# A list schedule for every engine, in place of program order, in a two-layer hybrid block

## The chip, the core and the metric

The kernel runs on one core of one Trainium2 chip. The metric is the device time of one execution in microseconds (us); the figure to go by is the median of a few runs. The core has a tensor engine (PE), a vector engine (DVE), a scalar engine (ACT), GpSimd (POOL), a sync engine (SP) that here issues nearly all loads, and 16 DMA engines. Each engine takes its instructions from a queue of its own, in order; semaphores make an instruction wait for work of another engine. A matrix product takes its operands from SBUF and accumulates in PSUM, of which the kernel keeps six tiles for its products: `mm_66` to `mm_69`, and the two larger ones `ax_70` and `ax_71`.

## The reference

Two layers work on 256 context tokens and 512 latent tokens, 1024 channels wide, all in float32. One input projection feeds three groups of heads side by side; their outputs are joined and projected; then comes an MLP. Each half ends in a gated residual and a LayerNorm. The second layer keeps only the latent tokens.

```python
def layer(x, c, ...):
    p = modulate(x, shift, scale) @ w_in             # one projection, split in three
    a = chunk_token_mlp(p_a)                         # gated token mixing in chunks of 128
    b = gqa(p_b)                                     # softmax attention, 6 query heads, rotary
    d = gated_delta_rule(conv(q), conv(k), conv(v))  # chunks of 64, a state passed on, two directions
    x = layer_norm(alpha * x + gate * (concat(a, b, d * gate_z) @ w_out))
    h = square(relu(modulate(x, ...) @ w_up))        # 1024 -> 4096
    return layer_norm(alpha * x + gate2 * (h @ w_down))
```

## The kernel before

**Tiles and stages.** Tokens go in groups of 128, channels in groups of 128. A float32 operand of a large product is split into a rounded half and a rest (`whi`, `wlo` for a weight; `xh`, `xl`, `x2xh`, `x2xl`, `hh`, `hl` for activations), and `mm3` (line 385) forms each product as three: high with high, high with low, low with high. ACT makes the rounded half and DVE the rest (`split`, line 381). So every weight goes from DRAM into `wraw`, then over ACT (`whi`) and DVE (`wlo`) to PE. Per layer the stages are: modulation and projection; convolutions and gates of the delta rule; three rounds `p` of `dn_prep` (a triangular inverse built by 31 dependent DVE steps), `makes` and `scans` of 64x64 products in the four quarters of the array (`kv,TT`, `S,rP`, `rwu,A`, `id,qd`, `kd,rwu`); attention beside them (scores `akh,qs` and `akl,qs` in an `ax` tile, transposes of `ape`, then `apT,ava`, the product of weights and values, on half of the array); the output projection; and the MLP, whose first product goes through the `mm` tiles and whose second collects in `ax_70` and `ax_71` and is added to `acc` by DVE.

**What sets the order.** Every engine call goes through `_Engine.call` (line 213), so all instructions carry L213 and are told apart by tile names. The stages are Python generators, and class `Flow` (line 30) runs them side by side: it keeps an estimated clock for each engine from hand-written costs, resumes the generator whose time is earliest (less `BIAS` for the delta-rule chains), and lends out PSUM tiles. So a generator writes its instructions in small bunches. What comes out is one program order, which the tile framework's own priorities turn into the engines' queues. PSUM tiles and buffers are assigned there, while the program is written.

```python
            for s in self.live:
                t = self.when(s)
                if t is not None and (best is None or (t - s[5], s[1]) < best[:2]):
                    best = (t - s[5], s[1], t, s)
```

Of the kernel before, what the change touches and what calls it, by code (L numbers as in the profile page):

```python
# [9 lines left out]
F32R = mybir.dt.float32r  # L10
# [3 lines left out]
PSUM = bass.MemoryType.PSUM  # L14
DRAM = bass.MemoryType.DRAM

P = 128
# [22 lines left out]
class Flow:  # L40
# [8 lines left out]
    def __init__(self, tc):  # L49
        self.tc = tc  # L50
        self.free = {}
        self.ready = {}
        self.done = {}
        self.live = []
        self.count = 0
        self.last = 0.0
        self.slots = {}
        self.spare = {}
        self.lent = {}
# [7 lines left out]
    @staticmethod  # L67
    def width(a):
        n = 1
        for s in a.shape[1:]:  # L70
            n *= s
        return n
# [150 lines left out]
            setattr(self, k, _Engine(flow, k, getattr(nc, k)))  # L223


def _tb(v):

    return 1 - v if v < 2 else 7 - v
# [62 lines left out]
class K:  # L291
    def __init__(self, ctx, tc, d, dump=None):
        self.tc = tc
        self.flow = Flow(tc)
        self.nc = _Core(tc.nc, self.flow)
        self.d = d
        self.dump = dump
        self.ctx = ctx
        self.open_ = []


    def open(self, name, side="left", space=None):
        kw = {} if space is None else {"space": space}
        cm = self.tc.tile_pool(name=name, bufs=1, side=side, reuse_waits="tile", **kw)
        p = cm.__enter__()
        self.open_.append((p, cm))
        return p

    def close(self, *pools):
        for p in pools:  # L310
            i = next(i for i, (q, _) in enumerate(self.open_) if q is p)
            self.open_.pop(i)[1].__exit__(None, None, None)

    def setup(self):
        nc, tc, ctx, d = self.nc, self.tc, self.ctx, self.d
# [348 lines left out]
def _body(ctx, tc, d, out, dump=None, stop=None):  # L664
    K_ = Kernel(ctx, tc, d, dump)
    K_.run(out, stop)
    for p, cm in reversed(K_.open_):
        cm.__exit__(None, None, None)

# [17 lines left out]
class Kernel(K):  # L687
# [784 lines left out]
    def dn_make(self, l, p, v, qkv, G, A, TT, r):  # L1472
# [5 lines left out]
        kds, ks, egc, be, E = G["kds"], G["ks"], G["egc"], G["be"], G["E"]  # L1478
        hs = slice(2 * p, 2 * p + 2)
        td = (v, _tb(v))  # L1480
        a0 = 0 if l == 0 else 2
        he = lambda a: a.rearrange("p t (h e) -> p t h e", e=HD)
# [59 lines left out]
    def dn_scan(self, l, p, v, A, r, S, o):  # L1542

        nc, sc = self.nc, self.dn
        need = l == 0 or v > 1
        a0 = 0 if l == 0 else 2
        td = (v, _tb(v))
        mm = nc.tensor.matmul
        halves = [_half(f) for f in range(2)]
# [405 lines left out]
```

## Time and profile before

| | before |
|---|---|
| median of 3 runs | 2041.31 us (2038.36 to 2041.98) |
| profiled execution | 2039.17 us, span 2037.4 us |
| granted TensorE clock, mean | 0.950 |
| PE busy | 1859.2 us, 91% |
| DVE busy | 1284.2 us, 63% |
| ACT busy | 854.5 us, 42% |
| POOL busy | 279.2 us, 14% |
| DMA | 204.44 MB, mean 100 GB/s |
| chain that ended last | PE 61%, DVE 18%, issue 7%, ACT 5%, POOL 4%, DMA 3% |

Busy times are sums over instructions, with overlaps counted once; the profiled execution's own time is its span and about 2 us around it. By stages, in us from the span's start: modulation and projection of layer 0 to 104, convolutions and first delta-rule work to 309, mixers to 538, output projection to 616, MLP to 1179 (PE without a pause), layer 1's mixers to 1609, its output projection to 1663, its MLP to 2027, and a last LayerNorm to 2037.4. The granted clock is the share of full speed that TensorE was given: 1.00 is 2.4 GHz, and a stretch at 1.2 GHz counts as 0.5.

### The profile page before, as it was taken

Reading aid. Unit: us, or ns where it says so; the run is one execution under the profiler, and the core shown is the slowest. Engines: PE = TensorE matmul, PEld = TensorE weight load, DVE = VectorE, ACT = ScalarE, POOL = GpSimd, SP = SyncE. Lnnn points to the kernel's source line nnn. Section 1 sums busy time; section 2 is a strip of 40 time slices with the busy share of each in tenths; the row PEclk is TensorE's granted clock in tenths of the full one; section 3 lists DMA queues with packets and bytes.
Section 4 is the critical chain, followed back from the end, with each engine's and each line's share of the span. In section 5 each row is a group of like instructions: output and inputs, shape, how many; then the busy total and the mean of one; then the engine's idle time right before and its main releaser. Section 6 shows DMA issues by size and latency. Waiting matters only on the chain.

```text
span 2037.4 us, 35195 instructions
## 1 busy us (share of the span) xinstructions
PE 1859.2 (91%) x14496; PEld 1519.5 (75%) x14496; DVE 1284.2 (63%) x2165; ACT 854.5 (42%) x1607; POOL 279.2 (14%) x479
## 2 busy tenths in 40 slices
PE   6999887898898999999999989988778879999997
PEld 2778675566678878888888777877666668888886
DVE  4668786765587245464457776888785575544555
ACT  3434435456546322322232274443655545323331
POOL 1111215431021000000000111111522020000001
PEclk8989889989999999999999979987997989999999
DMA  8211015313326323242355242100000544322331
GB/s 284 93 58 50 27 37 175 120 31 118 107 96 226 99 83 115 83 155 74 113 165 185 84 147 89 62 29 21 27 27 6 189 164 136 103 83 83 114 104 52
DMA packets 74060, 204.44 MB, mean 100 GB/s; under 512 B 9730, under 2 KB 23938, under 8 KB 73900
## 3 DMA queue, kind: packets, MB, share of 16 engines
q1 hardware_dynamic: 62764, 184.51, 27.9%
q10 hardware_dynamic: 11136, 17.70, 2.3%
q8 instruction: 113, 1.85, 0.4%
q14 instruction: 47, 0.39, 0.1%
HBM read 184.38 MB, written 17.79 MB: 99 GB/s over the span
## 4 chain that ended last, share of the span: by engine, by line
PE 61%; DVE 18%; issue 7%; ACT 5%; POOL 4%; DMA 3%; SPq 0%; ACTq 0%; POOLq 0%; DVEq 0%
PE mm L213 37%; PE ax L213 25%; DVE cacc L213 2%; DVE Xx L213 2%; DVE tm L213 2%; DVE wlo L213 2%; POOL crn L213 2%; DVE M L213 1%; DMA wraw<-in_w_up 1%; POOL rs L213 1%; DVE anm L213 1%; ACT ape L213 1%; DVE st L213 1%; POOL arn L213 1%; ACT osq L213 1%
## 5 line engine op out<-in xcount | busy, mean ns | idle before, releaser
L213 ACT ACTIVATE whi<-wraw 128x1024 fp32r<-128x1024 f32 (+2 forms) x188 | 194.6, 1050 | 443.1 <-PE ax L213 287.7
L213 DVE TENSOR_TENSOR wlo<-wraw,whi 128x1024 fp32r<-128x1024 f32 (+2 forms) x188 | 226.6, 1212 | 236.5 <-ACT whi L213 235.7
L213 PE MATMUL mm<-x2xh,whi 128*128 128x256 f32 (+1 forms) x832 | 287.7, 346 | 12.3 <-ACT whi L213 11.2
L213 PE MATMUL mm<-x2xl,whi 128*128 128x256 f32 (+1 forms) x832 | 287.0, 345 | 0.0
L213 PE MATMUL mm<-x2xh,wlo 128*128 128x256 f32 (+1 forms) x832 | 285.4, 343 | 0.7 <-DVE wlo L213 0.7
L213 PE MATMUL ax<-whi,hh 128*128 128x512 f32 x640 | 251.4, 393 | 0.1
L213 PE MATMUL ax<-wlo,hh 128*128 128x512 f32 x640 | 250.2, 391 | 0.0
L213 PE MATMUL ax<-whi,hl 128*128 128x512 f32 x640 | 250.1, 391 | 0.0
L213 PEld LDWEIGHTS mm<-x2xh,whi 128*128 128x128 f32 x832 | 159.7, 192 | 34.6 <-ACT whi L213 12.0
L213 DVE TENSOR_TENSOR acc<-acc,ax 128x1024 f32<-128x1024 f32 x68 | 83.0, 1220 | 148.3 <-PE ax L213 148.2
L213 PEld LDWEIGHTS mm<-x2xh,wlo 128*128 128x128 f32 x832 | 159.0, 191 | 20.0 <-DVE wlo L213 1.1
L213 PEld LDWEIGHTS mm<-x2xl,whi 128*128 128x128 f32 x832 | 159.7, 192 | 17.5
L213 PEld LDWEIGHTS ax<-whi,hh 128*128 128x128 f32 x640 | 120.2, 188 | 29.6 <-ACT hh L213 5.6
L213 PEld LDWEIGHTS ax<-whi,hl 128*128 128x128 f32 x640 | 120.2, 188 | 27.3 <-DVE hl L213 2.9
L213 PEld LDWEIGHTS ax<-wlo,hh 128*128 128x128 f32 x640 | 120.3, 188 | 26.9 <-issue 2.6
L213 POOL TENSOR_SCALAR rs<-mv 128x1 f32<-128x1 f32 x52 | 33.1, 638 | 702.6 <-DVE mv L213 701.4
L213 DVE SCALAR_TENSOR_TENSOR acc<-modw,cz,acc 128x1024 f32<-128x1024 f32 x80 | 101.2, 1282 | 7.6 <-DMA acc<-in_mod_b 4.6
L213 ACT ACTIVATE rl<-mm 128x256 f32<-128x256 f32 (+1 forms) x104 | 50.7, 490 | 131.4 <-PE mm L213 131.4
L213 POOL MEMSET acc<- 128x1024 f32 x10 | 9.5, 955 | 468.9 <-PE mm L213 468.9
L213 DVE TENSOR_TENSOR hl<-rl,hh 128x768 fp32r<-128x768 f32 (+2 forms) x76 | 54.5, 717 | 29.7 <-ACT hh L213 29.7
L213 DVE TENSOR_REDUCE anm<-ax 128x1 f32<-128x768 f32 (+1 forms) x60 | 50.6, 848 | 33.3 <-PE ax L213 33.2
L213 DVE SCALAR_TENSOR_TENSOR cacc<-cb,cw,cacc 128x772 f32<-128x772 f32 (+1 forms) x72 | 70.0, 975 | 0.7 <-ACT cacc L213 0.2
(255 smaller groups left out, 4127.1 us busy)
## 6 DMA issues: line engine op xcount, KB each, us to landing
modw<-in_mod_w SPq DMA_DIRECT2D x80, 512.0 KB
wraw<-in_w_up SPq DMA_DIRECT2D x64, 512.0 KB
wraw<-in_w_down SPq DMA_DIRECT2D x64, 512.0 KB
wraw<-in_w_ch SPq DMA_DIRECT2D x22, 512.0 KB
modw<-in_mod_w SPq DMA_DIRECT2D x32, 256.0 KB
wraw<-in_w_out SPq DMA_DIRECT2D x16, 512.0 KB
x_d<-xt ACTq DMA_DIRECT2D x16, 512.0 KB
xt<-x_d SPq DMA_DIRECT2D x14, 512.0 KB
```

Source lines behind the costliest of these rows:

```text
L213: return f(*args, **kw)
```

## The change

When the whole program is written, a new class `Order` goes over it once more. It takes all instructions, builds the graph of what must precede what (`graph`, from the memory that each reads and writes, from PSUM tiles and from the buffers of pools, whose openings and closings new wrappers record), gives each a cost (`costs`), and works out the longest path from each to the end (`tail`). `schedule` then simulates the engines and fills each one's queue: of the instructions that are ready, the one with the longest path to the end goes first. On PE two rules are added. Products on disjoint parts of the array that have the same operand names (one kind) form a unit and are issued one behind the other (`units`). And among the first `LOOK` (16) candidates, one of the same kind as the last product gets a bonus of `STICK` (5000 ns of path). No instruction, tile, shape or buffer is added, removed or altered; the order on each engine's queue is fixed by dependencies without semaphores.

```diff
+    SAME, OTHER = 110.0, 220.0
+    LOOK, STICK, LATE, SWITCH = 16, 5000.0, 20.0, 250.0
...
+        for i in pe:
+            x = self.ins[i]
+            self.kind[i] = tuple(a.bass_ap.tensor.name.split("_")[0].rstrip("0123456789") for a in (*x.ins, *x.outs) if hasattr(a, "bass_ap"))
+            part = len(self.cells[i]) < 16
+            if unit and (not part or used & set(self.cells[i]) or any(newest(j) > unit[0] and j not in unit for j in self.pred[i]) or self.kind[i] != self.kind[unit[0]]):
+                close()
+                unit, used = [], set()
...
+    def schedule(self, key):
...
+            elif e == E.PE:
+                some = [heapq.heappop(avail[e]) for _ in range(min(len(avail[e]), self.LOOK))]
+                worth = lambda c: (c[0] - self.STICK * (self.kind[c[1]] == last) + self.LATE * max(0.0, max(cell[q] for q in self.cells[c[1]]) - t), c[1])
+                pick = min(some, key=worth)
...
+            else:
+                k, i = heapq.heappop(avail[e])
...
+    def apply(self):
+        far = self.tail()
+        out = self.schedule([-f for f in far])
+        dep = mybir.DependencyInfo(mybir.DependencyClass.NoSync, mybir.DependencyReason.DATA)
+        for e, seq in out.items():
+            for a, b in zip(seq, seq[1:]):
+                self.tc.add_manual_dep(self.ins[b], self.ins[a].name, dep)
...
 def _body(ctx, tc, d, out, dump=None, stop=None):
     K_ = Kernel(ctx, tc, d, dump)
     K_.run(out, stop)
+    Order(tc, K_.pools).apply()
```

**First place.** PE in the projection of layer 0, around the product of the delta rule's gates `g` with the triangle `tri`. A row is a position in the queue, the tile written, its operands, the tile's shape and how many in a row. Before:

```order
226 L213 MATMUL mm_66<-xh,wlo 128x256
227 L213 MATMUL mm_68<-xh,whi 128x512
228 L213 MATMUL mm_68<-xl,whi 128x512
229 L213 MATMUL mm_68<-xh,wlo 128x512
230 L213 MATMUL mm_69<-g,tri 128x36 x4
231 L213 MATMUL ax_70<-tri,g 6x128 x6
232 L213 MATMUL mm_66<-xh,whi 128x256
```

And after the change:

```order
253 L213 MATMUL mm_67<-xh,wlo 128x512
254 L213 MATMUL mm_66<-xh,wlo 128x256
255 L213 MATMUL mm_68<-xh,wlo 128x512
256 L213 MATMUL mm_66<-xh,whi 128x256
257 L213 MATMUL mm_68<-xh,whi 128x512
258 L213 MATMUL mm_69<-g,tri 128x36 x4
259 L213 MATMUL mm_67<-g,c_sel 128x72
260 L213 MATMUL mm_66<-xl,whi 128x256
```

The gate products stand 28 rows further back, behind projection products that before stood behind them; and products into several PSUM tiles take turns where before one tile's three came together.

**Second place.** PE in the attention of layer 0, around the product `apT,ava`. Before:

```order
1829 L213 MATMUL mm_68<-c_ident,ape 128x128 x4
1830 L213 MATMUL mm_67<-c_ident,ape 128x128 x2
1831 L213 MATMUL ax_71<-akh,qs 128x512
1832 L213 MATMUL ax_71<-akl,qs 128x512
1833 L213 MATMUL mm_69<-apT,ava 64x128 x11
1834 L213 MATMUL mm_66<-c_ident,ape 128x128 x4
```

And after:

```order
1619 L213 MATMUL mm_69<-apT,ava 64x128 x2
1620 L213 MATMUL ax_70<-akh,qs 128x512
1621 L213 MATMUL mm_69<-apT,ava 64x128 x2
1622 L213 MATMUL ax_70<-akl,qs 128x512
1623 L213 MATMUL mm_69<-apT,ava 64x128 x2
1624 L213 MATMUL ax_70<-akh,qs 128x256
```

What was a run of eleven products on half of the array has become pairs with score products on the whole array between them.

**Third place.** PE near the end of the last MLP, where one pair of `ax` tiles is finished and the next begun. Before, one tile at a time:

```order
8472 L213 MATMUL ax_71<-whi,hh 128x512
8473 L213 MATMUL ax_71<-wlo,hh 128x512
8474 L213 MATMUL ax_71<-whi,hl 128x512
8475 L213 MATMUL ax_71<-whi,hh 128x512
8476 L213 MATMUL ax_70<-wlo,hh 128x512
```

And after:

```order
8134 L213 MATMUL ax_71<-whi,hl 128x512
8135 L213 MATMUL ax_70<-whi,hl 128x512
8136 L213 MATMUL ax_71<-whi,hh 128x512
8137 L213 MATMUL ax_71<-wlo,hh 128x512
8138 L213 MATMUL ax_71<-whi,hl 128x512
8139 L213 MATMUL ax_71<-whi,hh 128x512
8140 L213 MATMUL ax_71<-wlo,hh 128x512
8141 L213 MATMUL ax_71<-whi,hl 128x512
8142 L213 MATMUL ax_70<-whi,hh 128x512
8143 L213 MATMUL ax_71<-whi,hh 128x512
```

The two tiles of a pair now take turns, so both are complete within six products, and the next use of `ax_71` (row 8143) stands one product behind its last one (row 8141). On DVE the last LayerNorms of the tokens stood one behind the other; before:

```order
1907 L213 TENSOR_TENSOR acc<-acc,ax_71 128x1024
1908 L213 BN_STATS st<-acc 128x6 x2
1909 L213 BN_AGGR mv<-st 128x2
1910 L213 SCALAR_TENSOR_TENSOR xt<-acc,mv,lg 128x1024
1911 L213 SCALAR_TENSOR_TENSOR xt<-xt,rstd,lb 128x1024
1912 L213 TENSOR_TENSOR acc<-acc,ax_70 128x1024
```

And after:

```order
1821 L213 TENSOR_TENSOR acc<-acc,ax_71 128x1024
1822 L213 BN_STATS st<-acc 128x6
1823 L213 TENSOR_TENSOR acc<-acc,ax_70 128x1024
1824 L213 BN_STATS st<-acc 128x6 x3
1825 L213 BN_AGGR mv<-st 128x2 x2
1826 L213 SCALAR_TENSOR_TENSOR xt<-acc,mv,lg 128x1024 x2
1827 L213 SCALAR_TENSOR_TENSOR xt<-xt,rstd,lb 128x1024 x2
```

The two last tokens are now handled together, step by step, so that all of the last token's steps but one half of the other's statistics stand behind the last evacuation.

Counted over the whole queue of PE: the units that other products interrupt go from 35 to 0; the places where one product uses another shape of the array, or another way through it, than the product before it go from 618 to 651, among them the exits from a run of `apT,ava` from 51 to 97, while changes between rounded-float32 products and transposes go from 164 to 123. Counted over the 78 times that an `ax` tile of a projection back to the residual is used again: before, the products that stand between its last product and its next use were never less than 11; now 27 of the 78 have so few between them that they run in under 2 us, 6 of these in under 1 us.

## Rows read from the trace of the kernel before

**Rows 1.** Granted clock of the whole span

```profile
core 0: 2037.4 us, clock 0.950
```

**Rows 2.** Stages: length, busy PE, PEld, DVE, ACT, POOL; clock, DMA share, GB/s

```profile
309.00:538.00 229.00, 194.38 (x3303) 141.59 (x3302) 146.94 (x354) 130.99 (x368) 74.02 (x158) 0.93 0.33 107
...
636.00:1179.00 543.00, 543.00 (x2821) 458.27 (x2820) 292.42 (x283) 156.87 (x219) 18.16 (x23) 1.00 0.37 120
1179.00:1427.00 248.00, 218.24 (x1502) 185.61 (x1500) 193.56 (x413) 123.41 (x214) 43.94 (x59) 0.89 0.21 69
...
1673.00:2027.00 354.00, 353.09 (x1632) 293.06 (x1630) 184.47 (x181) 128.11 (x184) 7.09 (x8) 1.00 0.32 102
...
sum 2037.40, PE 1859.25 PEld 1519.51 DVE 1284.19 ACT 854.54 POOL 279.24; mean PE 143.02 PEld 116.89 DVE 98.78 ACT 65.73 POOL 21.48
```

**Rows 3.** Timeline of PE: start, length, product, idle time before and its releaser

```profile
87.65 1.04 PE L213 MATMUL mm<-g,tri 128*128 128x36 f32 x7 [2.83 <-issue]
...
228.82 0.66 PE L213 MATMUL mm<-c_ident,axn 128*128 128x128 f32 x2 [6.20 <-DVE axn L213]
...
317.15 1.76 PE L213 MATMUL mm<-kv,TT 64*64 64x128 f32 x14 [8.13 <-DVE kv L213]
...
621.86 0.58 PE L213 MATMUL mm<-x2xh,whi 128*128 128x256 f32 x1 [5.53 <-ACT whi L213]
...
1329.70 0.33 PE L213 MATMUL mm<-wlo,xmxh 128*128 128x128 f32 x1 [2.32 <-DVE wlo L213]
...
1528.23 0.80 PE L213 MATMUL ax<-akh,qs 128*128 128x512 f32 x1 [3.21 <-ACT ape L213]
...
1668.50 0.58 PE L213 MATMUL mm<-x2xh,whi 128*128 128x256 f32 x1 [4.02 <-ACT whi L213]
```

**Rows 4.** Timeline of DVE and of ACT before two of these products

```profile
87.36 0.30 DVE L213 SCALAR_TENSOR_TENSOR g<-gpo,ea 128x36 f32<-128x36 f32 x2
...
1666.33 1.17 ACT L213 ACTIVATE v<-mm,sh,sc 128x128 f32<-128x128 f32 x3
1667.36 1.09 ACT L213 ACTIVATE whi<-wraw 128x1024 fp32r<-128x1024 f32 x1
```

**Rows 5.** Timeline of PE where kinds and shapes alternate

```profile
440.42 0.28 PE L213 MATMUL mm<-id,qd 64*64 64x64 f32 x4
440.53 0.28 PE L213 MATMUL mm<-A,rwu 64*64 64x64 f32 x4
...
442.33 0.51 PE L213 MATMUL ax<-akh,qs 128*128 128x512 f32 x1
442.76 0.45 PE L213 MATMUL mm<-S,rP 64*64 64x64 f32 x8
443.14 0.51 PE L213 MATMUL ax<-akl,qs 128*128 128x512 f32 x1
443.57 0.28 PE L213 MATMUL mm<-rwu,A 64*64 64x64 f32 x2
```

**Rows 6.** Page, costliest groups: addition of an `ax` tile; busy, mean ns, idle before

```profile
L213 DVE TENSOR_TENSOR acc<-acc,ax 128x1024 f32<-128x1024 f32 x68 | 83.0, 1220 | 148.3 <-PE ax L213 148.2
```

**Rows 7.** Timeline of PE, last two products

```profile
2026.51 0.39 PE L213 MATMUL ax<-wlo,hh 128*128 128x512 f32 x1
2026.74 0.39 PE L213 MATMUL ax<-whi,hl 128*128 128x512 f32 x1
```

**Rows 8.** Timeline of DVE, last token

```profile
2027.17 1.22 DVE L213 TENSOR_TENSOR acc<-acc,ax 128x1024 f32<-128x1024 f32 x1 [0.69 <-PE ax L213]
2028.42 1.29 DVE L213 BATCH_NORM_STATS2 st<-acc 128x6 f32<-128x512 f32 x2
2029.74 0.21 DVE L213 BATCH_NORM_AGGREGATE mv<-st 128x2 f32<-128x12 f32 x1
2029.99 1.28 DVE L213 SCALAR_TENSOR_TENSOR xt<-acc,mv,lg 128x1024 f32<-128x1024 f32 x1
2031.99 1.28 DVE L213 SCALAR_TENSOR_TENSOR xt<-xt,rstd,lb 128x1024 f32<-128x1024 f32 x1 [0.71 <-POOL rstd L213]
```

More of the change, by code (lines that the diff above doesn't have):

```diff
@@ new lines, with __init__, size, tile @@
+class Pools:
+    def __init__(self):
+        self.events = []
+class _Pool:
+    def __init__(self, pools, pool, side):
+        self.pools, self.pool, self.side, self.tags = pools, pool, side, {}
+        pools.events.append(("open", self))
+    def size(self):
+        return sum(b * n for b, n, _ in self.tags.values())
+    def tile(self, shape, dtype, tag=None, bufs=1, name=None):
+        kw = {} if tag is None else {"tag": tag}
+        t = self.pool.tile(shape, dtype, bufs=bufs, name=name, **kw)
+        tag = tag or name
+        n = 4 * math.prod(shape[1:])
+        n = -(-n // 32) * 32
+        b, k, names = self.tags.get(tag, (0, 0, []))
+        names.append(t.tensor.name if hasattr(t, "tensor") else t.name)
+        self.tags[tag] = max(b, n), max(k, bufs), names
+        return t
@@ L299, in __init__ @@
         self.open_ = []
+        self.pools = Pools()
     def open(self, name, side="left", space=None):
@@ L304, in open @@
         cm = self.tc.tile_pool(name=name, bufs=1, side=side, reuse_waits="tile", **kw)
-        p = cm.__enter__()
+        p = _Pool(self.pools, cm.__enter__(), side)
         self.open_.append((p, cm))
@@ L312, in close @@
             self.open_.pop(i)[1].__exit__(None, None, None)
+            self.pools.events.append(("close", p))
     def setup(self):
```

322 lines of the change are left out of this document (added).

## The prediction

> **What bounds the kernel now.** I read the busy shares first, then the table by stages, then the idle times of the tensor engine, and last the ends of both MLPs. The bound is the tensor engine: it is busy 1859.2 of 2037.4 us, DVE 1284.2, ACT 854.5 [rows 2]. An order can gain only where PE stands still or runs more slowly than it could, so the first number is its idle time, 2037.4 - 1859.2 = 178 us. The stages tell where it lies. The two MLPs have none: 543.00 of 543.00 us and 353.09 of 354.00, at a granted clock of 1.00 [rows 2]. The mixers have much: 229.00 - 194.38 = 34.6 us in layer 0's, 248.00 - 218.24 = 29.8 us in the first part of layer 1's, at clocks of 0.93 and 0.89 [rows 2]. The whole span has a clock of 0.950 [rows 1]; if a stretch at 1.2 GHz counts as 0.5, then 2 x 0.05 x 2037.4 = 204 us ran at that level.
>
> The third view says what PE waited for. Some waits have one product at the head of the queue whose input is late, with others behind it that need nothing of the kind. The gate product at 87.65 waits 2.83 us. The page says "issue", but DVE makes `g` only at 87.36, and ends it at 87.66: PE waited for that [rows 3, 4]. The product before the second MLP waits 4.02 us for a split weight, which ACT starts at 1667.36 behind other activations without a pause [rows 3, 4]. Others are chains: `kv` comes 8.13 us late, and nothing in the order of PE mends that [rows 3]. The new order of PE keeps four `kv,TT` products ahead of those waits and 48 behind, so I leave it at zero.
>
> **The change part by part.** No product is removed or added, so the sum is made of waits that are covered, waits that are new, changes of the array's shape, and the end.
>
> *Waits covered.* Six of the rows are of the kind that a better order covers: 2.83 (`g,tri`, with 28 rows more ahead of it after the change), 6.20 (`axn`, 65 products more ahead), 5.53 and 4.02 (first weights of the MLPs; the second one's ACT split now stands ahead of nine other activations), 2.32 (`wlo`, 35 products more ahead) and 3.21 (scores behind an `ape` transpose, 48 more ahead): 24.1 us together [rows 3]. The weight of the MLP in layer 0 may be late because its load is, so I take 22 of them. Of the 178 us, these six, the 8.13 of `kv` and the last 10 us of the span, where PE has nothing left (its last product starts at 2026.74 [rows 7]), leave 136 us in many short waits. From 0 to all of them could go. Most are ends of chains with little ready behind them, so I choose an eighth, 17 us, with 0 and half of them, 68, as the ends. Covered: 22 + 17 = 39 us.
>
> *Units and shapes.* Two products of different names and one shape follow at 0.11 us, as `id,qd` and `A,rwu` do at 440.42 and 440.53. Where the shape changes, a score product comes 0.43 us before the next start (442.33 to 442.76, and 443.14 to 443.57), while products of 512 columns that follow each other are 0.23 us apart (2026.51 to 2026.74) [rows 5, 7]. So a change of shape costs 0.2 us and a change of name nothing. The 35 units that were broken up and are whole now would give 35 x 0.2 = 7 us if a change of name cost as much as one of shape. By the rows they give 0. The Trainium skill, TensorEngine Tiling (Array Packing), section Key Properties, says the same: changing the tiling mode, "not just tile", drains the engine; by it too the units are worth nothing, and pairing score products with half-array products costs. The trace agrees, at 0.43 against 0.23 us.
>
> Against this stands what the order loses: exits from `apT,ava` go from 51 to 97, 46 x 0.2 = 9.2 us. All changes of shape or way go from 618 to 651, because 41 changes between products and transposes vanish. At half of the 0.2 us each, since the rows show none of these, they give back 4 us; at 1.2 GHz, which the mixers have in part, the 9.2 could be 16. I take +10, with ends of +5 and +16.
>
> *The `ax` tiles.* This is a wait that the change adds. Before, one `ax` tile was filled while the other was emptied, and at least 11 products lay between a tile's last product and its next use, 11 x 0.227 = 2.5 us. Emptying takes 1.22 us on DVE [rows 6], and from the start of the last product to the end of that addition pass 2028.39 - 2026.74 = 1.65 us, of which 0.39 is the product [rows 7, 8]: 1.26 us from its end. Now both tiles of a pair are full nearly at once, and 27 of 78 places have under 2 us between them, six under 1 us. Behind the waiting product on PE stand all products of the next pair: nothing else is ready in an MLP's last part, and PE has no idle time there that could take it [rows 2]. If DVE is free, the wait is 1.26 us less the cover: 1.03 us at the place of one product shown, and about 4 us over the ten shortest. If DVE has other splits ahead, or empties the other tile first, one more addition of 1.22 us comes on top, at worst at all 27: 33 us. DVE is busy 292 of 543 us in the first MLP, so it is free nearly half of the time. I take +5, with ends of 0 and +33; a gain is excluded, since PE does not wait there now.
>
> *The end.* After the last product DVE takes 1.22 (addition), 1.29 (statistics), 0.21, 1.28, a wait of 0.71 and 1.28, and its last step ends at 2033.27, 6.14 us after the product's end at 2027.13 [rows 7, 8]. In the new order the other token's steps lie between: one addition, three halves of statistics (1.94), two of 0.21, and four of 1.28, so 1.22 + 1.94 + 0.42 + 5.12 = 8.7 us. The other token's addition and first half (1.22 + 0.65) begin when its tile is full, six products or 1.36 us earlier, and push this by 0.5, and gaps between instructions by 0.2: 9.4 us, so +3.3 us. The wait of 0.71 is covered. I take +3, with ends of 0 and +5.
>
> *Transfers and the other engines.* SP's loads are reordered too; at the start loads of `modw` go first and constants later. This is hidden where PE waits for `modw` anyway. I cost it at 0, with ends of -3 and +5, from the idle times of this size in the rows [rows 3]. Splits taken ahead on ACT and DVE displace activations by one or two slots of about 1 us; that cover is PE's longer queue of ready products.
>
> *Sum.* -39 + 10 + 5 + 3 = -21 on the profiled execution's own 2039.2 us: 2018 us. That execution lies 2.1 us under the median of the runs, 0.1%, which I don't correct for; I say 2019.
>
> **The rivals.**
>
> *Bunching costs more than the gaps give (slower).* Place: the 27 short reuses of an `ax` tile. If each costs one addition, that is 33 us, the shapes cost 16 and the end 3: 52 against 39 covered, +13, so 2052 us. It decides as soon as the three together pass 39 us, which at 16 and 3 is 20 us of new waits, 0.74 us at each of the 27 places. For it: DVE takes additions one behind the other, the two tiles now come together, and the MLPs have no slack on PE. Against it: DVE is free 46% of the first MLP, and most of the 27 have 1.3 to 2 us of cover, over the 1.26 us of an undisturbed emptying.
>
> *The gaps reopen (no change).* In the first part of layer 1 DVE is busy 193.56 of 248.00 us [rows 2], and its steps there are serial. Products taken ahead into a gap are missing later, while the chain ends when it ended before. If half of the 39 returns, -39 + 19.5 + 18 = -1.5: 2038 us. For it: the 8.13 us for `kv`, which no order of PE covers [rows 3]. Against it: the longest path goes first now, so DVE's chains start earlier too.
>
> *The clock comes along (much faster).* About 204 us run at 1.2 GHz, all outside the MLPs, in stages with idle time [rows 1, 2]. If the share of idle time that is covered, 39 of 178 or 22%, brings the same share of these 204 us to 2.4 GHz, then 45 us become 22: 2019 - 22 = 1997 us. For it: stages with a clock of 1.00 are those without pauses. Against it: longest paths and clock needn't meet, and new waits in the MLPs would do the reverse.
>
> *The change doesn't do what it says.* The rows of the two orders exclude that for PE and DVE; I give it nothing.
>
> **How the numbers follow.** A measurement of this kernel tells about 0.2%, 4 us, from no change. The forecast (2003 to 2035) has 0.46, the clock (under 2003) 0.08, reopened gaps (2035 to 2045) 0.14, and bunching (over 2045) 0.32. Faster than 2037.2 takes the first two and a little of the third: 0.55. Within 4 us gets 0.11, slower 0.34. The range leaves out half of the clock's case below and a little of bunching's above, where waits at all 27 places meet fewer covered gaps: 1998 to 2058 us.
>
> **What would show it.** Right, if PE's idle time falls to about 140 us outside the MLPs, the products of the six rows show under 1 us of idle time, `apT,ava` and score products alternate with starts 0.4 us apart, and DVE's last step ends about 9.4 us after the last product. Wrong in the `ax` step, if the MLP stages show PE idle by over 10 us with products waiting for the addition of `ax` to `acc`; wrong in the covered waits, if DVE is the releaser of as much idle time in the mixers as now; wrong on the shapes, if the mixers' PE busy time doesn't rise.

## The result: slower by 1.5%, and the profile after

| | before | after |
|---|---|---|
| median | 2041.53 us (4 runs, one more than in the first table) | 2070.23 us (4 runs, 2067.40 to 2075.65) |
| ratio, 95% interval | | 1.0147 [1.0124, 1.0170] |
| profiled execution, span | 2039.17, 2037.4 us | 2075.65, 2073.7 us |
| PE busy, idle | 1859.2, 178.2 us | 1893.5, 180.2 us |
| mean granted clock | 0.950 | 0.943 (other runs 0.945 to 0.949) |

The profiled execution is the longest of the four, so its 36.3 us stand against 28.7 us between the medians. The first reading is in the table above: PE stands idle as long as before (2.0 us more), and is busy 34.3 us longer with the same products.

The clock has a part in those 34.3 us. Of its busy time PE spent 164.7 us in stretches at 1.2 GHz before and 182.6 after. A 512-column product there takes 0.42 us from start to start (1638.60 to 1639.02 in the trace after), and 0.23 at 2.4 GHz (1639.74 to 1639.97). If all products take about twice as long there, half of that time is lost to the clock: 82.3 and 91.3 us. What is left is PE's busy time at full speed, an estimate: 1776.9 before and 1802.2 after. So 25.3 of the 36.3 us are dearer products, 9.0 the clock and 2.0 idle time. The 9.0 may be mostly the choice of execution: the profiled one after the change has the lowest clock of its four, and the medians differ by 7.6 us less.

Where that lies, the table by stages shows. Its stretches are cut at the same products in both kernels: the first product of each output projection, the last product of each MLP, and the end. Columns: stretch, length, busy PE, PEld, DVE, ACT and POOL with counts, clock, DMA share, GB/s. Before:

```profile
0.00:538.40 538.40, 459.36 (x5118) 350.71 (x5118) 360.15 (x818) 260.25 (x575) 122.18 (x224) 0.92 0.30 99
538.40:1179.40 641.00, 629.48 (x3234) 528.47 (x3235) 369.56 (x389) 202.85 (x301) 37.47 (x48) 0.99 0.38 123
1179.40:1609.50 430.10, 363.97 (x4291) 303.97 (x4288) 315.48 (x705) 234.17 (x500) 101.59 (x183) 0.90 0.19 60
1609.50:2027.10 417.60, 406.42 (x1856) 336.36 (x1856) 233.72 (x248) 157.27 (x233) 16.18 (x22) 0.98 0.34 110
2027.10:2035.60 8.50, 0.03 (x1) 0.00 (x0) 5.29 (x6) 0.00 (x0) 1.83 (x2) 0.70 0.31 123
```

The same stretches after:

```profile
0.00:545.20 545.20, 473.57 (x5118) 356.52 (x5118) 362.70 (x819) 261.45 (x575) 125.92 (x224) 0.92 0.30 97
545.20:1188.60 643.40, 633.48 (x3238) 532.45 (x3239) 361.41 (x382) 199.10 (x306) 34.78 (x46) 0.99 0.37 121
1188.60:1636.30 447.70, 378.37 (x4287) 310.94 (x4285) 322.99 (x715) 230.22 (x494) 114.40 (x185) 0.88 0.19 61
1636.30:2060.60 424.30, 408.09 (x1856) 334.21 (x1856) 227.30 (x242) 152.88 (x231) 15.41 (x20) 0.98 0.32 105
2060.60:2072.30 11.70, 0.00 (x1) 0.00 (x0) 8.65 (x11) 0.00 (x0) 3.46 (x4) 0.59 0.22 90
```

The stretches grow by 6.8, 2.4, 17.6, 6.7 and 3.2 us. In the mixers of layer 0 PE is busy 14.2 us longer (459.36 to 473.57) and idle 7.4 less; in those of layer 1 it is busy 14.4 longer and idle 3.2 more. So 28.6 of the 34.3 us are in the two mixer stretches.

The products that take longer are those of the mixers, the small ones most. PE's timeline after, in the mixers of layer 0 (start, length, product, how many in a row):

```profile
433.87 0.68 PE L213 MATMUL mm<-kd,rwu 64*64 64x64 f32 x16
434.39 0.28 PE L213 MATMUL mm<-id,qd 64*64 64x64 f32 x4
434.60 0.38 PE L213 MATMUL ax<-akh,qs 128*128 128x256 f32 x1
434.91 0.33 PE L213 MATMUL mm<-A,rwu 64*64 64x64 f32 x4
435.08 0.28 PE L213 MATMUL mm<-id,qd 64*64 64x64 f32 x4
435.29 0.44 PE L213 MATMUL mm<-apT,ava 128*64 128x128 f32 x4
435.66 0.33 PE L213 MATMUL mm<-A,rwu 64*64 64x64 f32 x4
```

And before, the same kinds:

```profile
439.65 0.27 PE L213 MATMUL mm<-rwu,kd 64*64 64x64 f32 x2 [0.18 <-ACT rwu L213]
439.67 0.27 PE L213 MATMUL mm<-kd,rwu 64*64 64x64 f32 x2
439.72 0.25 PE L213 MATMUL mm<-rwu,kd 64*64 64x64 f32 x2
...
440.12 0.23 PE L213 MATMUL mm<-kd,rwu 64*64 64x64 f32 x2
440.18 0.23 PE L213 MATMUL mm<-id,qd 64*64 64x64 f32 x2
```

Two things are to be seen. Before, `rwu,kd` and `kd,rwu` take turns, 32 instructions in 0.53 us (439.65 to 440.18), since by the kernel's code one kind uses two quarters of the array and the other kind the other two. After, 16 `kd,rwu` alone take 0.52 us (433.87 to 434.39): half the rate, in two quarters. Both stretches ran at 2.4 GHz. And `id,qd` with `A,rwu`, which before came every 0.11 us [rows 5], now have a product of another shape between them, so that one round takes 0.69 to 0.74 us.

Summed over the whole trace, each product from its start to the next start on PE (or to the end of the work under way, if that is earlier) and at full speed as above:

| us at full speed | before | after |
|---|---|---|
| `kd,rwu` and `rwu,kd` | 21.6 | 31.6 |
| `id,qd` and `A,rwu` | 30.5 | 39.9 |
| `apT,ava` and the scores | 99.3 | 108.0 |
| transposes of `ape` | 41.9 | 44.1 |
| all products | 1776.9 | 1802.2 |

I read the first row as the parting of the two kinds by their quarters, and the second as the products of another shape in between; the third and fourth are those whose changes of shape the forecast priced. The rest of the products change by little each.

The waits came out as follows (engine and what it waited for, total, times, longest):

```profile
PE mm L213 <- ACT whi L213: 16.8, 4, 11.1
PE ax L213 <- ACT ape L213: 12.7, 15, 2.2
PE mm L213 <- DMA modw<-in_mod_w: 11.7, 7, 4.5
```

Of the seven waits of [rows 3] four are gone before the same product, counted within its kind (2.83, 8.13, 2.32, 3.21), and 6.20, 5.53 and 4.02 fell to 2.01, 1.16 and 1.74. That is 27 us of waits gone. As many came in elsewhere: in the two mixer stretches DVE released 79.1 us of PE's idle time before and 53.6 after, but ACT 52.7 and 69.8. The largest is one wait of 11.1 us, 1.8 before, at the first product of layer 1's output projection:

```profile
1636.32 1.22 PE L213 MATMUL mm<-whi,yh 128*128 128x512 f32 x2 [11.08 <-ACT whi L213]
```

SP's queue shows one cause: the loads of `w_out` stand behind loads of `y`, which wait for the last heads' output.

```profile
1594.45 26.04 SPq L213 DMA_DIRECT2D y<-y_d  x4
...
1623.81 2.01 SPq L213 DMA_DIRECT2D y<-y_d  x2
1627.16 5.40 SPq L213 DMA_DIRECT2D wraw<-in_w_out  x3
```

In the kernel before the same three loads stand ahead of the load of `y` at 1604.43:

```profile
1592.68 1.75 SPq L213 DMA_DIRECT2D wraw<-in_w_out  x3
```

Last, the MLPs and the end. The MLPs run with little idle time: 0.9 and 2.7 us before, 3.5 and 4.7 after (length less busy PE; before first, then after):

```profile
621.80:1179.30 557.50, 556.56 (x2905) 471.02 (x2906) 303.73 (x296) 163.97 (x231) 20.15 (x25) 0.99 0.38 123
1668.40:2027.00 358.60, 355.90 (x1640) 295.50 (x1640) 188.98 (x186) 130.78 (x188) 7.09 (x8) 0.99 0.32 105
```

```profile
623.60:1188.70 565.10, 561.63 (x2930) 474.27 (x2931) 304.75 (x303) 174.91 (x270) 22.87 (x28) 0.99 0.38 123
1698.40:2060.70 362.30, 357.58 (x1640) 294.39 (x1640) 179.65 (x177) 126.97 (x190) 4.96 (x6) 0.99 0.31 98
```

Of the 4.5 us more, one wait of 1.09 us is for the addition of an `ax` tile, at the third place shown, where the tile's reuse is row 8136, one product behind row 8134 (row 8143 goes on with the tile and waits for nothing):

```profile
2046.71 0.50 PE L213 MATMUL ax<-whi,hh 128*128 128x512 f32 x1 [1.09 <-DVE acc L213]
```

Nine others of 0.3 to 0.5 us in layer 1's MLP (3.5 us) are put down to ACT's `hh`, and the largest in layer 0's (1.9) to ACT's `rl`.

The end on DVE after, which answers to [rows 8]:

```profile
2059.28 1.22 DVE L213 TENSOR_TENSOR acc<-acc,ax 128x1024 f32<-128x1024 f32 x1 [3.30 <-PE ax L213]
2060.54 0.69 DVE L213 BATCH_NORM_STATS2 st<-acc 128x6 f32<-128x512 f32 x1
2061.15 1.20 DVE L213 TENSOR_TENSOR acc<-acc,ax 128x1024 f32<-128x1024 f32 x1
2062.27 1.87 DVE L213 BATCH_NORM_STATS2 st<-acc 128x6 f32<-128x512 f32 x3
2064.06 0.32 DVE L213 BATCH_NORM_AGGREGATE mv<-st 128x2 f32<-128x12 f32 x2
2064.30 2.46 DVE L213 SCALAR_TENSOR_TENSOR xt<-acc,mv,lg 128x1024 f32<-128x1024 f32 x2
2067.48 2.48 DVE L213 SCALAR_TENSOR_TENSOR xt<-xt,rstd,lb 128x1024 f32<-128x1024 f32 x2 [0.71 <-POOL rstd L213]
```

Both tokens' steps stand together, and the last ends at 2069.96, 9.4 us after the last product's end at 2060.6.

### The profile page after: what moved, and what is told of

Its sections match the earlier page's. It is cut to its first block, busy times and chain, and to the rows that moved or that the text cites. A ratio compares the mean times of both kernels' runs of the same rounds, so it can differ in the third digit from the quotient of the medians.

```text
span 2073.7 us, 35243 instructions
## 1 busy us (share of the span) xinstructions
PE 1893.5 (91%) x14496; PEld 1534.1 (74%) x14496; DVE 1283.1 (62%) x2165; ACT 843.7 (41%) x1605; POOL 294.0 (14%) x479
## 5 line engine op out<-in xcount | busy, mean ns | idle before, releaser
L213 PE MATMUL mm<-x2xh,whi 128*128 128x512 f32 (+1 forms) x832 | 211.6, 346 | 5.6 <-ACT v L213 2.1
L213 PE MATMUL ax<-whi,hh 128*128 128x512 f32 x640 | 207.4, 394 | 4.9 <-ACT hh L213 3.6
L213 PE MATMUL mm<-x2xl,whi 128*128 128x512 f32 (+1 forms) x832 | 209.3, 343 | 0.0
L213 PE MATMUL mm<-x2xh,wlo 128*128 128x512 f32 (+1 forms) x832 | 207.6, 343 | 0.0
L213 PE MATMUL ax<-wlo,hh 128*128 128x512 f32 x640 | 204.8, 390 | 0.2 <-DVE wlo L213 0.2
L213 PE MATMUL ax<-whi,hl 128*128 128x512 f32 x640 | 201.4, 390 | 0.0
L213 PEld LDWEIGHTS mm<-x2xl,whi 128*128 128x128 f32 x832 | 144.2, 191 | 19.3
L213 PEld LDWEIGHTS ax<-wlo,hh 128*128 128x128 f32 x640 | 119.2, 188 | 24.1 <-DVE wlo L213 0.7
L213 DVE SCALAR_TENSOR_TENSOR acc<-modw,cz,acc 128x1024 f32<-128x1024 f32 x80 | 100.1, 1279 | 17.6 <-DMA acc<-in_mod_b 9.9
L213 ACT ACTIVATE rl<-mm 128x512 f32<-128x512 f32 (+1 forms) x104 | 49.7, 495 | 126.5 <-PE mm L213 125.6
L213 PE MATMUL mm<-whi,yh 128*128 128x512 f32 x160 | 58.7, 404 | 16.6 <-ACT whi L213 12.9
L213 ACT ACTIVATE v<-mm,sh,sc 128x128 f32<-128x128 f32 x152 | 57.4, 465 | 37.1 <-PE mm L213 29.5
```

What stands on the lines that cost most here:

```text
L213: return f(*args, **kw)
```

## The experiments

Each ran on one chip with the kernel before; the ratio is to that. Busy and idle time and the clock are of the profiled execution. "At full speed" is PE's busy time less half of what lies in stretches at 1.2 GHz, the estimate of above.

| | median us | ratio to before, interval | PE busy | at full speed | PE idle | clock |
|---|---|---|---|---|---|---|
| before | 2041.53 | 1 | 1859.2 | 1776.9 | 178.2 | 0.950 |
| after | 2070.23 | 1.0147 [1.0124, 1.0170] | 1893.5 | 1802.2 | 180.2 | 0.943 |
| e1_pe_only | 2144.01 | 1.0497 [1.0471, 1.0524] | 1887.6 | 1800.9 | 261.0 | 0.936 |
| e2_all_but_pe | 2145.72 | 1.0498 [1.0473, 1.0522] | 1906.3 | 1791.8 | 238.4 | 0.929 |
| e3_no_bonus | 2080.24 | 1.0174 [1.0147, 1.0200] | 1889.8 | 1814.3 | 181.4 | 0.952 |
| e4_bonus_by_shape | 2079.92 | 1.0183 [1.0159, 1.0207] | 1882.3 | 1785.7 | 193.5 | 0.938 |
| e5_units_by_shape | 2050.86 | 1.0056 [1.0035, 1.0077] | 1859.2 | 1776.9 | 193.2 | 0.945 |
| e7_shape_and_w_out | 2055.68 | 1.0085 [1.0065, 1.0104] | 1861.1 | 1774.2 | 191.3 | 0.941 |
| e8_no_units | 2053.49 | 1.0072 [1.0051, 1.0093] | 1878.5 | 1807.4 | 174.3 | 0.954 |
| e9_before_kd_apart | 2046.74 | 1.0026 [1.0012, 1.0040] | 1868.3 | 1780.1 | 178.3 | 0.946 |
| e10_by_tile | 2049.36 | 1.0042 [1.0026, 1.0058] | 1858.7 | 1768.7 | 189.7 | 0.940 |
| e11_by_tile_w_out | 2050.01 | 1.0048 [1.0033, 1.0064] | 1853.2 | 1770.9 | 192.1 | 0.944 |
| e12_three_queues | 2049.82 | 1.0035 [1.0021, 1.0049] | 1852.6 | 1773.0 | 192.9 | 0.947 |
| e13_and_no_units | 2040.00 | 0.9993 [0.9977, 1.0008] | 1862.5 | 1782.0 | 172.6 | 0.948 |

**Halves of the change.** The first two ask which engines' order carries the loss.

```diff
         for e, seq in out.items():
+            if not (e == mybir.EngineType.PE):   # e1; e2 has != here
+                continue
```

> The new order is imposed on PE's queue alone; the other queues go back to the framework's own priorities. Theory (the loss is in PE's own order: more time per product, since kinds are bunched and array shapes alternate): about 2065, between 2055 and 2075, PE busy near 1893 as after the change. Rival (the loss comes from the new orders of DVE, ACT and SP, which make PE wait elsewhere): 2045 or less, PE busy still near 1890 but idle under 165.

> The new order is imposed on DVE, ACT, POOL and SP, and not on PE, whose queue goes back to the framework's priorities. Counted over the queue, changes of array shape fall back to the number of before (574 against 581 before and 620 after, counted by array cells), and alternations of kd,rwu with rwu,kd to 274 (475 before, 14 after). Theory (loss in PE's own order): PE busy about 1865, time 2040 to 2050. Rival (loss in the other engines' orders): 2060 to 2075.

Both came out at 2144 to 2146 us, far slower than the whole change, so both theories missed. My reading, not tested, is that orders of engines that were planned together don't fit others: PE's idle time is 261 us in e1 (2148.6 - 1887.6) and 238 in e2 (2144.7 - 1906.3). The two don't tell the halves apart. e1 does show PE's products as dear as in the whole change, 1800.9 us at full speed.

**The bonus.**

```diff
-    LOOK, STICK, LATE, SWITCH = 16, 5000.0, 20.0, 250.0
+    LOOK, STICK, LATE, SWITCH = 16, 0.0, 20.0, 250.0
```

> STICK is 0: no bonus for the kind of the last product; units stay. Theory (bunching by names parts products that would run in different quarters of the array, worth about 10 us; but without a bonus shapes change 783 times instead of 620, worth about 9 us): no real change, 2065 to 2072, the 64x64 products cheaper by 10 us and the changes dearer by as much. Rival 1 (the bonus alone is the loss): 2041 to 2050. Rival 2 (the bonus is useful, what harms lies elsewhere): over 2080.

2080.24 us is at the edge of the second rival, but the ratios to before, 1.0174 here and 1.0147 for the change, have intervals that overlap, so the time doesn't show whether the bonus is of use. The products do: at full speed they cost 12.1 us more than with it. `kd,rwu` and `rwu,kd` are 2.7 us cheaper (28.9), as the theory has it, but the transposes of `ape` 9.1 dearer (53.2) and `apT,ava` and the scores 4.6 (112.6).

```diff
-                worth = lambda c: (c[0] - self.STICK * (self.kind[c[1]] == last) + ...
+                worth = lambda c: (c[0] - self.STICK * (self.shape(c[1]) == last) + ...
...
+    def shape(self, i):
+        return self.round[i], bool(self.ins[i].is_transpose), len(self.cells[i])
```

> The bonus goes to a product of the same array shape and way (rounded float32, transpose or plain float32; a quarter, half or the whole of the array) instead of the same operand names. Shape changes fall to 528 (620 after the change, 581 before), alternations of kd,rwu with rwu,kd rise from 14 to 90. Theory (time per product is the loss): summing the pitches that the two traces show for each pair of neighbours gives 1717 us against 1733 after the change and 1708 before, so 15 us less: about 2055. Rival (time is lost in waits, not in pitches): 2065 to 2075.

PE's products came out 16.5 us cheaper at full speed, as the theory's 15, but the time did not follow: 2079.92. The mixers of layer 0 became shorter (545.2 to 539.3 us); over the whole span PE's idle time rose by 13.3 us, 9.3 of them in layer 1's mixers (69.3 to 78.6), and the clock, 0.938, took 5.3 more.

**Units of four quarters.** The kind is the shape in the bonus and in the units, so a unit holds `kd,rwu` and `rwu,kd` in all four quarters. The same edit reaches a third use of the kind, the price `SWITCH` that the simulation puts on a change of kind on the same cells.

```diff
-            self.kind[i] = tuple(a.bass_ap.tensor.name.split("_")[0]...
+            self.kind[i] = (self.round[i], bool(x.is_transpose), len(self.cells[i]))
```

> Kind is the array shape for both rules, the bonus and the units, so that a unit holds four 64x64 products of two names in the four quarters of the array (kd,rwu with rwu,kd). These alternate 537 times (14 after the change, 90 in e4_bonus_by_shape, 475 before) and shapes change 492 times (620 after, 581 before). The pitches that the traces show, summed over this order, give 1708 us as before the change, 24 us less than after it. Theory (PE's time per product is the loss): PE busy about 1868, time about 2046, 2040 to 2055. Rival (what PE saves there it stands idle instead, since the chains on the other engines set the end): PE busy under 1875, but 2065 to 2080.

PE is busy 1859.2 us, as before the change to the tenth, and the time is 2050.86: 19 us of the 29 are back. The timeline of PE shows the kinds in turns again, with 32 instructions in 0.51 us:

```profile
434.61 0.27 PE L213 MATMUL mm<-kd,rwu 64*64 64x64 f32 x1
434.61 0.27 PE L213 MATMUL mm<-rwu,kd 64*64 64x64 f32 x1
434.62 0.27 PE L213 MATMUL mm<-kd,rwu 64*64 64x64 f32 x1
...
435.12 0.29 PE L213 MATMUL mm<-id,qd 64*64 64x64 f32 x4
```

The theory holds for the products: at full speed they take 1776.9 us as before the change, 25.3 less than after it. The two kinds take 20.1 (31.6 after), and `id,qd` with `A,rwu` 34.6 (39.9): the edit mends the parted quarters and some of the changes of shape together. The mixers now take 538.9 and 432.6 us, 0.5 and 2.5 more than before. The rival has a part too: PE's idle time is 193.2 us, 13.0 more than after the change. These 15.0 us over before are all that the profiled execution has over it.

**One pair of kinds, in the kernel before.** The same cost by itself:

```diff
         for d, h in blk:
             for i, f in enumerate(halves):
                 mm(ps[f, ...], wu[f, d, h, 0:HD], kd[f, d, h], start=True, stop=True)
+        for d, h in blk:
+            for i, f in enumerate(halves):
                 e = i if d == 0 else 1 - i
                 ...
```

> The kernel before, with one loop of dn_make written as two: all eight rwu,kd products of a block, then all eight kd,rwu, instead of one of each in turn. Same products, but now eight in a row use two quarters of the array where before four quarters took turns. Theory (parting these two kinds costs what the traces show for them: 23.6 us between starts before the change, 36.1 us after it): about 12 us slower than before, 2048 to 2058 if before is at 2041. Rival (the mixers' idle time on PE takes it up): within 4 us of before.

Ratio 1.0026 [1.0012, 1.0040], about 5 us. PE is busy 9.1 us more, of which 5.9 are the clock; at full speed its products take 3.2 us more, and the two kinds 26.0 where they took 21.6. A block in the trace:

```profile
442.76 0.51 PE L213 MATMUL mm<-kd,rwu 64*64 64x64 f32 x10
443.06 0.27 PE L213 MATMUL mm<-rwu,kd 64*64 64x64 f32 x2
443.10 0.28 PE L213 MATMUL mm<-kd,rwu 64*64 64x64 f32 x3
```

Ten of one kind take 0.30 us, the rate of two quarters. So the mechanism is shown, at under half of the size expected: behind these rows the kinds still take turns. In the order of starts they change 270 times in the whole trace, 896 before and 122 after the change. The interval, 2 to 8 us, does not exclude the rival's 4, but its reason is not there: PE's idle time, 178.3 us, takes nothing up.

**Units at all.**

```diff
-            if len(unit) > 1:
+            if False:
```

> The order of the change without units; the bonus for a kind stays. Shapes change 651 times instead of 620. Theory (units by names are worth nothing or little): 2070 to 2076. Rival (units keep quarters of the array busy together and are worth the 13 us that the summed pitches give): 2080 or more.

The other way round from both: 2053.49 us, by the ratios 15 us faster than with units by names. PE is busy 15 us less, and the clock is higher in every run, 0.950 to 0.958 against 0.943 to 0.949. In the profiled execution 20.3 us are gained by the clock (142.1 us of the busy time at 1.2 GHz, 182.6 after the change) and 5.9 by less idle time, while the products are 5.2 us dearer at full speed. So here nearly all of the gain is in the clock.

**The wait before the projection.** e6 was the change with the three loads of `w_out` moved ahead on SP, with 2061 us expected if the 11.1 us wait comes from their place in that queue, and 2070 if not. It has no time: in this order the engines' queues wait for each other in a circle. e7 is e5 with the same move.

```diff
+        w = [i for i in out[E.SP] if of(i) == "in_w_out"][8:11]
+        sp = [i for i in out[E.SP] if i not in w]
...
+        out[E.SP] = sp[:at] + w + sp[at:]
```

> Both edits. If both theories hold they add up: about 2037, 2030 to 2045, no slower than before the change. If time saved in products turns into waits: 2055 to 2070.

2055.68, no gain, and by the ratios some 6 us over e5. The loads are issued from 1595.39 to 1598.18, some 17 us ahead of their splits; but ACT's queue has `yh` ahead of these, and the wait of PE is still 9.1 us:

```profile
1614.72 0.52 ACT L213 ACTIVATE yh<-y 128x384 fp32r<-128x384 f32 x1 [7.26 <-DMA y<-y_d]
1615.15 2.94 ACT L213 ACTIVATE whi<-wraw 128x1024 fp32r<-128x1024 f32 x3
```

e10 first keeps the accumulations of one tile together:

```diff
-            self.kind[i] = (self.round[i], bool(x.is_transpose), len(self.cells[i]))
+            self.kind[i] = (..., x.outs[0].bass_ap.tensor.name if self.round[i] else None)
```

> e5_units_by_shape with one edit: for rounded-float32 products the kind also names the PSUM tile, so that the bonus keeps one tile's accumulation together as before the change, and ax tiles no longer fill in pairs (5 of 78 reuses with under 2 us of cover, 25 in e5). Theory (pairs of ax tiles cost the end 3 to 4 us and the MLPs little): last product to end 8.5 us instead of 12.7, 2044 to 2048 where e5 had 2051. Rival (pairs cost nothing that is not hidden): 2051.

2049.36: no clear gain over e5's 2050.86, and the last stretch takes 11.7 us, not 8.5, since DVE's queue still mixes the two last tokens. On that point the theory missed the cause: it is the order of DVE. e11 moves the loads on SP again and the splits on ACT ahead of the last `yh`; e12 does the same on DVE with `wlo` and `yl`.

```diff
+        out[E.Activation] = act[:y] + c + act[y:]      # e11: c are the three whi
...
+        out[E.DVE] = dve[:y] + c + dve[y:]             # e12: c are the three wlo
```

> e10_by_tile, with the first three loads of w_out of layer 1 as early in SP's queue as before the change (as in e7_shape_and_w_out) and their three splits on ACT ahead of the last yh, behind which they stood in e7. Theory (both queues together made PE's 9 to 11 us wait before that projection): the wait falls to under 3 us, the time by 6 to 8 us against e10, to about 2039. Rival (the projection waits for the last heads' output anyway): the wait stays, with another releaser, and the time is that of e10.

> e11_by_tile_w_out, and on DVE too the three wlo of w_out of layer 1 stand ahead of the last yl, behind which they stood in e11. Theory (SP, ACT and DVE each held these weights behind the last heads' output, so that freeing one or two queues only moved the wait to the next): PE's wait of 8 to 9.7 us before that projection falls to under 4 us, and the time by about 5 us against e11, to 2042 to 2046 if before is at 2040. Rival (the wait moves once more, to y itself): under 2 us of gain, 2049 or more.

In e11 ACT's three splits come at 1605.98, and PE starts two products; then it waits for `wlo`, which on DVE stands behind `yl`:

```profile
1614.24 0.56 DVE L213 TENSOR_TENSOR yl<-y,yh 128x384 fp32r<-128x384 f32 x1 [8.23 <-ACT yh L213]
1614.72 3.49 DVE L213 TENSOR_TENSOR wlo<-wraw,whi 128x1024 fp32r<-128x1024 f32 x3
```

```profile
1607.09 0.73 PE L213 MATMUL mm<-whi,yh 128*128 128x512 f32 x2 [2.13 <-ACT whi L213]
1615.99 0.80 PE L213 MATMUL mm<-wlo,yh 128*128 128x512 f32 x1 [8.18 <-DVE wlo L213]
```

In e12 the projection begins after a wait of 1.8 us, but then PE waits 6.4 us for the next weights, whose loads stand behind three more of `y` on SP (issued from 1613.05):

```profile
1620.02 1.22 PE L213 MATMUL mm<-whi,yh 128*128 128x512 f32 x2 [6.43 <-ACT whi L213]
```

e11 and e12 have the same time, 2050. So the rivals were right on the time: the wait moved from queue to queue, three times. No run freed all of it, so what the 11.1 us are worth is not shown.

The last run is e12 with the edit of e8, units left out.

```diff
-            if len(unit) > 1:
+            if False:
```

> e12_three_queues without units. Theory (what e8_no_units gained, 17 us, it gained by the granted clock, 0.950 to 0.958 against 0.943 to 0.949 after the change, while its products take longer at full clock): clock over 0.948 and time 2030 to 2042. Rival (units of shape keep the quarters of the array busy together, and that is worth more here): PE busy over 1865, 2046 or more.

2040.00 us, 0.9993 [0.9977, 1.0008] of before: 30 us faster than the change, and as fast as before. The time is in the theory's range, but the clock isn't what gave it: it is 0.938 to 0.949, and 0.940 to 0.947 in e12, and PE is busy 10 us more than there. PE's idle time gave it, 172.6 us against 192.9, under the 178.2 of before. Both mixers show it (e12 first, then e13):

```profile
0.00:530.40 530.40, 457.26 (x5119) 349.92 (x5119) 360.67 (x819) 261.24 (x575) 123.68 (x224) 0.93 0.30 100
1177.80:1606.40 428.60, 356.52 (x4283) 295.94 (x4281) 323.79 (x714) 230.36 (x494) 113.77 (x185) 0.90 0.18 58
```

```profile
0.00:511.10 511.10, 446.45 (x5119) 341.53 (x5119) 359.21 (x819) 260.40 (x575) 120.65 (x224) 0.95 0.31 104
1162.40:1600.50 438.10, 373.94 (x4283) 308.64 (x4281) 322.60 (x714) 231.19 (x494) 113.04 (x185) 0.88 0.19 60
```

Layer 0's mixers gain 19 us, in idle time (73.1 to 64.7) and clock; layer 1's lose 10, in the clock and 5.7 us of dearer products, though their idle time falls too (72.1 to 64.2). Without units the two kinds are mostly parted again, 29.4 us against 19.8 in e12, and all products cost 9.0 us more at full speed; the 20.3 us less idle time outweigh that. That units cost time is shown twice, 15 us in e8 against the change and 9 in e13 against e12, by the ratios. Why, is not: a unit is held until its last member is ready, which would fit the idle time of e13, while in e8 the clock has nearly all of it.

## Why the prediction was wrong, point by point

- **Forecast and rivals.** 2019 us (1998 to 2058) and faster; measured 2070.23 and slower. The slower rival, bunching, had the sign and the word, not the mechanism: its price was the reuse of `ax` tiles, which cost little. The sum was -39 + 10 + 5 + 3 = -21. The profiled executions differ by +36.3: idle time outside the MLPs and the end -5, products +25.3, MLPs +4.5, the end +2.8, and the clock +9.0, which had no term.
- **Waits covered, -39: the step that failed as a sum.** At their places most came as forecast: 24.1 us at the six products fell to 4.9 (three of them kept over 1 us, against the sign I had given), and even `kv` (8.13), put at zero, is gone. But PE's idle time went from 178.2 to 180.2, where the sum has about 147. I counted what a better order covers, and not what it uncovers: waits for DVE in the mixers fell by 25.5 us, those for ACT rose by 17.1. That was the rival of reopened gaps, to which I gave half of the sum and a chance of 0.14; 34 of the 39 came back.
- **Units and shapes, +10: the step that was mis-sized most.** The products cost 25.3 us more at full speed. The exits from `apT,ava`, priced at 9.2, came to 8.7 us at `apT,ava` and the scores; the transposes, which should have given 4 back, cost 2.2. What I had not priced came on top: 10.0 us at `kd,rwu` and `rwu,kd`, and 9.4 at `id,qd` and `A,rwu`. I read from [rows 5] that a change of name costs nothing, and so took kinds as equal; I did not ask which quarters the names stand for. e5 takes the whole 25.3 back by one edit, e9 shows a part of the first 10.0 alone. The Trainium skill, TensorEngine Tiling (Array Packing), section Key Properties, has the rule I passed over, next to the one I used: different tiles of the array can work in parallel. The trace agrees, with 32 instructions in 0.53 us over four quarters against 16 in 0.52 over two.
- **`ax` tiles, +5.** The number is right by luck: idle time in the MLPs rose by 2.5 and 2.0 us, but only 1.09 us of it waited for an addition, at the one place that I had worked out (1.03). The rest has other releasers, and the ten shortest reuses did not cost the 4 us.
- **The end, +3.** Right: from 8.5 to 11.7 us, and 9.4 us from the last product to DVE's last step.
- **Transfers and queues, 0.** Wrong by up to 11 us at one place. I gave `w_out` no row, since it waited only 1.8 us before. The change takes the buffers of `w_out` as free only when the whole of the pools under them is done, so it places the loads, the splits and the rests late in three queues. This is read from `graph`; no run changes that rule by itself.
- **The clock.** I had it as a gain (rival of 0.08), and it did not come: 0.943 to 0.949 after, with 0.939 to 0.951 in all runs of the kernel before.

## What to carry to other kernels

Where small products share the array, look at which cells each kind takes before putting kinds together: group by the shape of the array, and fill the cells that are free. Price an order by the time between starts of each pair of neighbours in the trace, not by a count of changes of one sort: from both traces this gave 24 us for the change, where 25.3 are measured at full speed, and named e5 as the repair. It prices the products alone: e8 and e13 have dearer products and are faster, by the clock and by idle time. And a list schedule puts every queue in order by one model: where the model is wrong about one buffer, all the queues hold the same work back, and mending one of them shows nothing.

## What was not expected of the hardware

The granted clock moved with the order by as much as the terms under dispute: from 0.938 (e4) to 0.954 (e8) with the same instructions. PE spent 193.1 us of its busy time at 1.2 GHz in e4 and 142.1 in e8, which by the estimate of above is 25.5 us of time. Over all runs of a kernel it was 0.935 to 0.938 in e4 and 0.950 to 0.958 in e8, with before at 0.939 to 0.951 between them; e5 and e10 had 0.940 to 0.945, and the much slower e2 0.926 to 0.929. I have not changed the clock by itself in any run, so what in an order moves it is open.
